# Attention over three branches: products of probabilities and values in plain float32, two heads on the halves of the array's columns

## The chip, the cores and the metric

The kernel runs on one core of a Trainium2 chip. A core has a matrix engine (TensorE; PE in the profile, PEld its weight loads) and four others: VectorE (DVE), ScalarE (ACT), GpSimd (POOL), and SyncE (SP), which here only issues DMAs. Each engine takes its instructions in the order in which the program gives them to it. The metric is the device time of one execution in microseconds, the median of the runs.

## What is computed

Two transformer blocks over 512 tokens of 1024 features, all in float32. The change touches the last attention of the second block. It has 16 heads of 64 features in four groups; the heads of a group share keys and values. Each head's result is a sum of three attentions, each times a gate of its own per token and head:

```python
o_cmp = einsum('bghqn,bngd->bqghd', p_cmp, v_cmp)     # 31 compressed blocks of the keys
o_sel = einsum('bghqkl,bgqkld->bqghd', p_sel, v_sel)  # selected blocks: with 512 keys, all of them
o_win = einsum('bghqs,bsgd->bqghd', p_w, v_w)         # the last 512 keys: all of them
out = einsum('bsch,bschd->bshd', gates, o).reshape(b, s, NSA_HEADS * DH)
return out @ w_o
```

With 512 keys, the second and the third are causal attentions over all earlier tokens, each with keys and values of its own.

## The kernel before

The weights stream in by large DMAs and are split into two parts, high and low, that TensorE's fast float32 (`float32r`) holds exactly; activations are split the same way (`split`, L542). A product of two float32 matrices is then three fast products (`group`, L556). All matmuls made by the helper `mm` bear its line, L540, so they are told apart by tiles and shapes.

The attention in question is `n_attend` (L2000). Its work is a list of steps, written out by hand: for each of four groups first one step for the compressed branch, then for each of four heads and each of two branches (`b`: selected, window) four steps, one for each chunk `c` of 128 queries in the order 3, 2, 0, 1. Chunk `c` meets 128 (c + 1) keys. That is 33 steps a group and 132 in all. A step has parts, and the table `ORDER` says how many steps after the step's scores each part is issued, and in which order the parts of different steps stand in the engines' queues:

- `scores` (L2081): two `float32r` products of queries and keys on TensorE, into one of three banks of PSUM;
- `bias` (L2089): on DVE the mask, the scale and the row's least value, into one of six buffers `np`;
- `exp` (L2097): on ACT the exponentials and their sum; `sums`: on DVE the reciprocal; `scale` (L2105): on POOL the probabilities times gate over sum;
- `turn` (L2111): on TensorE one to four transpositions, into one of four banks;
- `high` and `low` (L2119, L2128): the transposed probabilities as two parts, the high one made by ACT, the low one by DVE (tiles `pts` for branch 0, `pth` and `ptl` for branch 1);
- `out` (L2132): after a head's last chunk of a branch, eight products, four blocks of keys by two parts, 512, 384, 256 and 128 queries wide. The values stand on the 128 columns of the array as their high and low parts side by side (tile `vs`), so one product gives both. With branch 0 come two more, 512 wide, for the compressed branch (`cph`, `cpl`, `vc`). All sum up in one bank, `av`;
- `join` and `add` (L1761): ACT copies the lower half of that bank into the place of the head's queries (`h`), DVE adds the other half; `head` (L2156) makes the high part `oh` for each pair of heads. The low parts `ol` follow at the end of the stage (`lower`, L2013).

Beside the steps, `g_query` (L2054) prepares the queries of the next pair a little at each step ("tick"): a shuffle on DVE, the rotary embedding on POOL, the high part on ACT, the low part on POOL in two halves (L2075), and a DMA from SP's queue that copies them to the other half of the partitions. After the last step the output projection begins: the products of the first three pieces of the output weights (`out(k)`) are issued between the last parts of the steps.

Another place of the kernel, `g_pair` (L1013) in the first block, has plain float32 products with 64 columns of weights that go to the halves of a bank in turn (L1068, tiles `d` and `xc`).

Of the kernel before, what the change touches and what calls it, by code (L numbers as in the profile page):

```python
# [10 lines left out]
F32 = mybir.dt.float32  # L11
# [182 lines left out]
def _pcol(v):  # L194
    """A vector of 128 * n values as [128, n], value p of tile k at [p, k]."""
# [3 lines left out]
def _columns(x):  # L199
    """Per-partition columns: name -> [128, n]."""  # L200
# [25 lines left out]
def _constants():  # L226
    """Tables that depend on the shapes alone: name -> [128, n]."""
# [73 lines left out]
# ---------------------------------------------------------------- the kernel  # L301

class Weights:
    """The weight stream: large loads that run ahead, each piece split exactly in two parts."""
# [54 lines left out]
    def ahead(self):  # L359
        """The first half of what the next get() makes."""  # L360
# [10 lines left out]
class Norm:  # L371
    """One over the root of the mean square over the features, for tokens in the free dimension.

    The factor is applied to what the products give, so that they need not wait for it."""

    def __init__(self, s, eps, name, n=T, apart=False):
        """apart: the last squares are summed on their own."""
# [17 lines left out]
    def mean(self, src=None, more=None):  # L395
        """Mean squares with tokens on partitions, [128, chunks], before eps."""
# [32 lines left out]
    def bcast(self, tm=None, tag="rbc", bufs=2):  # L429
        """The factor along the free dimension, the same on every partition."""  # L430
# [13 lines left out]
class Norm2:  # L444
    """The norm that ends the first block and the one that opens the second, as one factor."""
# [22 lines left out]
class Kernel:  # L468
# [19 lines left out]
    def open_banks(self, stack, pool):  # L488
        """PSUM: a pool of eight banks, or banks by their places."""
# [66 lines left out]
    def group(self, ps, w, xh, xl, ks, first, last, m=P):  # L556
        """Accumulate into ps over the k tiles ks: three products of the parts."""
# [1695 lines left out]
```

## Time and profile before

| | |
|---|---|
| median of 3 runs (lowest, highest) | 2265.91 us (2264.5, 2266.25) |
| span of the profiled execution, first to last instruction | 2262.3 us; its own time beside the span is not given |
| PE busy | 2161.9 us (96%), 10250 instructions |
| PEld busy | 1776.0 us (79%) |
| DVE busy | 1305.9 us (58%), 2058 instructions |
| ACT busy | 910.6 us (40%), 1485 |
| POOL busy | 544.6 us (24%), 559 |
| chain that ended last, by engine | PE 68%, DVE 15%, ACT 7%, issue 5%, POOL 4%, DMA 1% |

Busy times are shares of the whole span, over stages of different kinds. A matmul's end is modelled, since matmuls are pipelined: a busy PE is not one at its peak. The chain is followed back from the last instruction, at each step to what released it. The attention that is changed begins at 1682.3 us of the span with its first scores; the first product of the output projection starts at 1850.88.

### The profile page before, as it was taken

What the parts mean: (1) busy time and instruction counts of PE and PEld (TensorE: products, weight loads), DVE (VectorE), ACT (ScalarE), POOL (GpSimd) and SP (SyncE); (2) the same over time, 40 slices, a digit from 0 to 9 for tenths busy, and PEclk for the clock granted to TensorE, in tenths of its full rate; (3) what the DMA queues carried; (4) which work ended last, traced back from release to release, by engine and by line L of the source; (5) the groups of instructions that cost most, each with busy time, mean ns of one, the idle gap of its engine ahead of it and who ended that gap; (6) DMA issues with size and microseconds to landing.
All of it is one profiled execution on the core that took longest, in us unless ns stands there. A gap on an engine that the chain in (4) does not pass through costs nothing.

```text
span 2262.3 us, 27154 instructions
## 1 busy us (share of the span) xinstructions
PE 2161.9 (96%) x10250; PEld 1776.0 (79%) x10250; DVE 1305.9 (58%) x2058; ACT 910.6 (40%) x1485; POOL 544.6 (24%) x559
## 2 busy tenths in 40 slices
PE   8899999999999999999899999999888899999998
PEld 5677888788888887777778888887677778888886
DVE  6988756454433335589965343445768875534333
ACT  4333534343322224366544332332448864423222
POOL 3333401111110104166630000013448851000001
PEclk9999999999999999999999999999899999999999
DMA  4222434122332223322233323323331113333231
GB/s 136 67 64 73 140 106 152 59 66 94 101 103 93 93 89 98 121 65 66 56 106 100 103 93 94 102 93 121 106 108 30 31 43 117 93 103 95 94 101 65
DMA packets 63379, 206.09 MB, mean 91 GB/s; under 512 B 7440, under 2 KB 8336, under 8 KB 63120
## 3 DMA queue, kind: packets, MB, share of 16 engines
q1 hardware_dynamic: 59504, 196.99, 27.8%
q10 hardware_dynamic: 3744, 7.37, 0.9%
q8 instruction: 80, 1.31, 0.2%
q14 instruction: 51, 0.42, 0.1%
HBM read 189.39 MB, written 6.29 MB: 86 GB/s over the span
## 4 chain that ended last, share of the span: by engine, by line
PE 68%; DVE 15%; ACT 7%; issue 5%; POOL 4%; DMA 1%; ACTq 0%; POOLq 0%; DVEq 0%
PE psum L540 53%; PE b L540 13%; DVE wl L350 2%; DVE spl L1718 1%; ACT wh L341 1%; DVE t L908 1%; POOL np L2108 1%; ACT sT L1670 1%; ACT sT L1671 1%; DVE pv L1089 1%; DVE xl L553 1%; POOL cx L1832 1%; PE psum L2116 1%; ACT xh L552 1%; DVE pts L2130 1%
## 5 line engine op out<-in xcount | busy, mean ns | idle before, releaser
L540 PE MATMUL psum<-xh,wh 128*128 128x512 f32 x1560 | 611.6, 392 | 2.3 <-ACT sA L1725 1.3
L540 PE MATMUL psum<-xh,wl 128*128 128x512 f32 x1560 | 609.4, 391 | 1.8 <-DVE wl L350 1.5
L540 PE MATMUL psum<-xl,wh 128*128 128x512 f32 x1560 | 608.8, 390 | 0.0
L341 ACT ACTIVATE wh<-ws 128x1024 fp32r<-128x1024 f32 (+1 forms) x346 | 356.3, 1038 | 384.8 <-PE psum L540 321.5
L350 DVE TENSOR_TENSOR wl<-ws,wh 128x1024 fp32r<-128x1024 f32 (+2 forms) x332 | 421.1, 1274 | 86.1 <-ACT wh L341 85.4
L540 PEld LDWEIGHTS psum<-xh,wl 128*128 128x128 f32 x1560 | 293.1, 188 | 66.3 <-DVE wl L350 4.3
L540 PEld LDWEIGHTS psum<-xh,wh 128*128 128x128 f32 x1560 | 293.3, 188 | 63.4 <-issue 1.8
L540 PEld LDWEIGHTS psum<-xl,wh 128*128 128x128 f32 x1560 | 293.3, 188 | 60.9 <-DVE xl L550 0.2
L540 PE MATMUL b<-xh,wh 128*128 128x512 f32 (+1 forms) x488 | 196.1, 402 | 8.4 <-ACT wh L341 6.6
L540 PE MATMUL b<-xh,wl 128*128 128x512 f32 (+1 forms) x488 | 193.6, 397 | 3.8 <-POOL wl L350 1.9
L540 PE MATMUL b<-xl,wh 128*128 128x512 f32 (+1 forms) x488 | 193.7, 397 | 0.5 <-DVE xl L553 0.5
L1357 DVE TENSOR_TENSOR h<-h,psum 128x512 f32<-128x512 f32 x48 | 33.1, 689 | 161.2 <-PE psum L540 161.2
L540 PE MATMUL psum<-hh,wh 128*128 128x512 f32 x320 | 125.1, 391 | 0.0
L540 PE MATMUL psum<-hh,wl 128*128 128x512 f32 x320 | 124.7, 390 | 0.0
L540 PE MATMUL psum<-hl,wh 128*128 128x512 f32 x320 | 124.6, 389 | 0.0
L1348 ACT ACTIVATE t<-t 128x512 f32<-128x512 f32 x64 | 40.5, 632 | 188.9 <-DVE t L1347 188.9
L540 PEld LDWEIGHTS b<-xh,wh 128*128 128x128 f32 (+1 forms) x488 | 92.9, 190 | 28.4 <-ACT wh L341 6.6
L540 PEld LDWEIGHTS b<-xh,wl 128*128 128x128 f32 (+1 forms) x488 | 92.8, 190 | 26.6 <-DVE wl L350 3.3
L553 DVE SCALAR_TENSOR_TENSOR xl<-h,cols,xh 128x512 fp32r<-128x512 f32 x64 | 76.6, 1212 | 61.9 <-ACT xh L552 61.9
L540 PEld LDWEIGHTS b<-xl,wh 128*128 128x128 f32 (+1 forms) x488 | 92.9, 190 | 20.5 <-DVE xl L553 1.2
L392 POOL TENSOR_TENSOR acc_final<-acc_final,sq_final 128x512 f32<-128x512 f32 x6 | 10.4, 1733 | 336.1 <-ACT sq_final L388 336.1
L1287 POOL TENSOR_TENSOR t<-t,t 128x512 f32<-128x512 f32 x22 | 28.4, 1290 | 257.2 <-DVE t L1282 232.7
(515 smaller groups left out, 3510.6 us busy)
## 6 DMA issues: line engine op xcount, KB each, us to landing
ws<-in_wst SPq DMA_DIRECT2D x332, 512.0 KB, 3.4
h<-in_xT SPq DMA_DIRECT2D x16, 256.0 KB, 3.7
kk<-kk SPq DMA_DIRECT2D x16, 256.0 KB, 3.4
nq<-nq SPq DMA_DIRECT2D x16, 256.0 KB, 2.9
ws<-in_wst SPq DMA_DIRECT2D x8, 384.0 KB, 3.1
spill<-back SPq DMA_DIRECT2D x8, 256.0 KB, 2.0
back<-spill ACTq DMA_DIRECT2D x8, 256.0 KB, 3.5
spill<-h ACTq DMA_DIRECT2D x8, 256.0 KB, 5.9
```

What stands on the lines that cost most here:

```text
L341: self.nc.scalar.activation(hi[:, :n], s, AF.Copy)
L350: e.tensor_tensor(lo[:, :n], s, hi[:, :n].bitcast(F32), op=ALU.subtract)
L540: self.nc.tensor.matmul(ps, a, b, start=start, stop=stop, skip_group_check=again)
L552: nc.scalar.activation(hi, src, AF.Copy, scale=scale)
L553: nc.vector.scalar_tensor_tensor(lo, src, scale, hi.bitcast(F32), op0=ALU.mult, op1=ALU.subtract)
L908: nc.vector.scalar_tensor_tensor(t, u[:, q:q + T], cw[:, q:q + 1], t, op0=ALU.mult, op1=ALU.add)
L1089: nc.vector.tensor_tensor(o[:, a:], src[:, a:], src[:, a - n:528 - n], op=ALU.add)
L1287: nc.gpsimd.tensor_tensor(t, t, gate[0], op=ALU.mult)
L1348: nc.scalar.activation(t, t, AF.Square)
L1357: nc.vector.tensor_tensor(self.h[:, m, :], self.h[:, m, :], ps, op=ALU.add)
L1670: self.nc.scalar.activation(t, t, AF.Exp)
L1671: self.nc.scalar.activation(t, t, AF.Ln, bias=1.0)
```

## The change

The products of probabilities and values become plain float32 products: the values are held once (64 columns), the probabilities too, and the two heads of a pair go to the two halves of the array's columns, and so to the halves of the bank `av`. The steps of a pair are put in the order branch, head, chunk, so that the two heads' probabilities of a branch are there together, and `out` is issued for both after the second head's last chunk. The transposed probabilities are copied out of PSUM once instead of split: chunks 3 and 0 by ACT, chunks 2 and 1 by DVE; three buffers take turns, one of them in the rest of the values' slab. A pair's result is split into `oh` and `ol` straight from the bank; joins, additions and the low parts at the end go. The low parts of the queries are made by DVE, in one instruction a head, instead of POOL in two. The compressed branch and the values before the steps lose their parts as well. The rest of the diff takes comments and docstrings out.

```diff
-        vs = self.slab("vs").rearrange("p k t -> p (k t)").rearrange(
-            "p (b c g d) -> p b c g d", b=2, c=4, g=4)
+        half = self.slab("vs", F32).rearrange("p k t -> p (k t)")
+        vs = half[:, :2048].rearrange("p (b c g d) -> p b c g d", b=2, c=4, g=4)
+        self.pt0 = half[:, 2048:3712].rearrange("p (n q) -> p n q", q=P)
...
         for c, ps in enumerate(pss):
-            o = self.vs[:, :, c, :, :]
-            v = ps.rearrange("p (b g d) -> p b g d", b=2, g=4)
-            for b in range(2):
-                self.split(o[:, b, :, 0:64], o[:, b, :, 64:128], v[:, b], norm.tm[:, c:c + 1])
+            nc.scalar.activation(self.vs[:, :, c, :, :],
+                                 ps.rearrange("p (b g d) -> p b g d", b=2, g=4), AF.Copy,
+                                 scale=norm.tm[:, c:c + 1])
...
-    ORDER = (("scores", 0), ("out", 7), ("join", 9), ("bias", 1), ("turn", 4), ("exp", 2), ("add", 9),
-             ("sums", 2), ("low", 6), ("tick", 0), ("high", 5), ("scale", 2), ("head", 13))
+    ORDER = (("scores", 0), ("out", 7), ("head", 9), ("bias", 1), ("turn", 4), ("exp", 2),
+             ("sums", 2), ("tick", 0), ("move", 5), ("scale", 2))
...
-            for h in range(4 * g, 4 * g + 4):
+            for h0 in (4 * g, 4 * g + 2):
                 for b in range(2):
-                    for c in self.QORD:
-                        steps.append(dict(g=g, h=h, b=b, c=c))
+                    for h in (h0, h0 + 1):
+                        for c in self.QORD:
+                            steps.append(dict(g=g, h=h, b=b, c=c))
...
-            if 0 <= j < 7:
-                lower(j)
-        lower(7)
...
             nc.scalar.activation(q[r, 0, :], qr[r, :], AF.Copy)
-            for s in halves:
-                nc.gpsimd.tensor_tensor(q[r, 1, s], qr[r, s], q[r, 0, s].bitcast(F32),
-                                        op=ALU.subtract)
-                yield
+            yield
+            nc.vector.tensor_tensor(q[r, 1, :], qr[r, :], q[r, 0, :].bitcast(F32),
+                                    op=ALU.subtract)
+            yield
...
-    def n_high(self, u):
+    def n_move(self, u):
...
+            self.pt[h, b] = self.pt0 if self.npt % 3 == 2 else self.tmp("pt", (P, 13, P), bufs=2)
+            self.npt += 1
+        dst = self.pt[h, b][:, c:4 * c + 1:3, :]
+        src = u.pop("ps")[:, :P * (c + 1)].rearrange("p (j q) -> p j q", q=P)
+        if c in (1, 2):
+            self.nc.vector.tensor_copy(dst, src)
+        else:
+            self.nc.scalar.activation(dst, src, AF.Copy)
...
-        if u["c"] != self.QORD[3]:
+        if u["c"] != self.QORD[3] or h % 2 == 0:
             return
-        pt = self.pt.pop((h, b))
+        halves = [slice(0, 64), slice(64, 128)]
         if b == 0:
             self.av = self.bank("av")
             cp, vc = self.cp
-            for part in cp:
-                self.mm(self.av, vc[:, h % 4, :], part, part is cp[0], False)
+            for e in range(2):
+                self.mm(self.av[halves[e]], vc[:, (h - 1 + e) % 4, :], cp, True, False)
+        pt = [self.pt.pop((h - 1 + e, b)) for e in range(2)]
         for j in range(4):
-            for part in pt:
-                self.mm(self.av[:, P * j:], self.vs[:, b, j, g, :],
-                        part[:, 4 * j:3 * j + 4, :].rearrange("p c q -> p (c q)"),
-                        False, b == 1 and j == 3 and part is pt[1])
+            for e in range(2):
+                self.mm(self.av[halves[e], P * j:], self.vs[:, b, j, g, :],
+                        pt[e][:, 4 * j:3 * j + 4, :].rearrange("p c q -> p (c q)"),
+                        False, b == 1 and j == 3)
...
             p = u["h"] // 2
-            self.nc.scalar.activation(self.oh[:, p, :], self.qraw[:, p, :], AF.Copy)
+            self.split(self.oh[:, p, :], self.ol[:, p, :], self.av)
```

## Rows read from the trace of the kernel before

**Rows 1.** Window: stretch, us, then busy us (instructions) of PE PEld DVE ACT POOL.

```profile
1718.02:1759.89 41.87, 36.84 (x239) 29.97 (x238) 37.04 (x145) 36.93 (x109) 34.96 (x55) 1.00 0.13 28
```

**Rows 2.** Waits of three groups: who waited for whom, us in total, times, longest.

```profile
PEld psum L2116 <- POOL np L2108: 15.2, 30, 0.8
DVE nsm L2103 <- ACT np L2099: 11.8, 15, 1.2
...
PEld psum L540 <- DVE pts L2130: 5.8, 12, 1.1
...
PEld psum L2116 <- POOL np L2208: 3.7, 3, 1.2
PEld psum L540 <- DVE ptl L2130: 3.3, 9, 0.7
```

**Rows 3.** DVE groups by shape, same stretch: busy us, mean ns, idle.

```profile
L2130 DVE TENSOR_TENSOR pts<-psum,pts 128x512 fp32r<-128x512 f32 x13 | 8.7, 673 | 0.0
...
L2130 DVE TENSOR_TENSOR pts<-psum,pts 128x384 fp32r<-128x384 f32 x12 | 6.5, 538 | 0.0
...
L2130 DVE TENSOR_TENSOR pts<-psum,pts 128x256 fp32r<-128x256 f32 x12 | 4.8, 403 | 0.0
...
L2130 DVE TENSOR_TENSOR pts<-psum,pts 128x128 fp32r<-128x128 f32 x12 | 3.2, 268 | 0.0
...
L1765 DVE TENSOR_TENSOR h<-h,psum 64x512 f32<-64x512 f32 x12 | 8.1, 678 | 0.5 <-ACT h L1764 0.3
```

**Rows 4.** ACT groups by shape, same stretch.

```profile
L2126 ACT ACTIVATE pts<-psum 128x384 fp32r<-128x384 f32 x13 | 6.1, 471 | 0.0
...
L2126 ACT ACTIVATE pts<-psum 128x256 fp32r<-128x256 f32 x12 | 4.6, 381 | 0.2
```

**Rows 5.** POOL groups by shape, same stretch.

```profile
L2075 POOL TENSOR_TENSOR nq<-qr,nq 64x256 fp32r<-64x256 f32 x23 | 16.8, 729 | 1.0
```

**Rows 6.** DVE groups, whole span: copies, subtractions on 64 partitions.

```profile
L941 DVE COPY btm<-b 128x384 f32<-128x384 f32 x2 | 1.1, 548 | 0.0
...
L1869 DVE COPY hidt<-psum 128x256 f32<-128x256 f32 x2 | 0.8, 411 | 0.0
...
L1455 DVE TENSOR_TENSOR sq<-st,sq 64x512 fp32r<-64x512 f32 x16 | 11.0, 686 | 1.2 <-ACT sq L1453 0.7
...
L1455 DVE TENSOR_TENSOR ks<-nkr,ks 64x512 fp32r<-64x512 f32 x8 | 7.6, 953 | 0.2
```

**Rows 7.** Timeline of DVE in the drain: start us, us of the piece.

```profile
1848.39 0.67 DVE L2014 TENSOR_TENSOR ol<-h,oh 128x512 fp32r<-128x512 f32 x1
1848.99 0.54 DVE L2130 TENSOR_TENSOR ptl<-psum,pth 128x384 fp32r<-128x384 f32 x1
```

**Rows 8.** Timeline of POOL, same moment.

```profile
1848.51 1.97 POOL L2108 TENSOR_SCALAR np<-np,nsm,gates 128x128 f32<-128x128 f32 x2
```

**Rows 9.** Timeline of PE: plain float32, 16 columns of the array, four products.

```profile
74.87 1.04 PE L540 MATMUL b<-small,adt 128*16 128x128 f32 x8
```

**Rows 10.** Timeline of PE: plain float32, halves of the columns, eight products (L1068).

```profile
99.23 0.39 PE L540 MATMUL b<-xl,wh 128*128 128x512 f32 x1
99.46 0.39 PE L540 MATMUL b<-xh,wl 128*128 128x512 f32 x1
99.78 1.09 PE L540 MATMUL b<-d,xc 128*64 128x128 f32 x16
100.80 0.94 PE L540 MATMUL b<-ct,prev 128*128 128x128 f32 x6
```

**Rows 11.** Timeline of PE: one head's products with the values, and what follows.

```profile
1777.62 0.39 PE L540 MATMUL psum<-cph,vc 128*128 128x512 f32 x1
...
1778.08 1.41 PE L540 MATMUL psum<-pts,vs 128*128 128x512 f32 x8
1779.32 0.30 PE L2116 MATMUL psum<-small,np 128*128 128x128 f32 x1
```

**Rows 12.** Timeline of PE in the drain.

```profile
1847.27 0.50 PE L540 MATMUL psum<-cph,vc 128*128 128x512 f32 x1 [1.46 <-DVE h L1765]
```

More of the change, by code (lines that the diff above doesn't have):

```diff
@@ L1797, in _nsa @@
         ):
-            self.oh = self.slab("oh")
-            pts = self.slab("pts").rearrange("p k t -> p (k t)")
-            self.pts = [pts[:, 1664 * a:1664 * a + 1664].rearrange("p (n q) -> p n q", q=P)
-                        for a in range(2)]
+            self.oh, self.ol = self.slab("oh"), self.slab("ol")
             self.n_attend()
@@ L1885, in second @@
                 self.mm(ps[:, :64], ht[:, e, :], w2[:, 1, e, :], e == 0, e == 1)
-            v = self.vcs
-            nc.scalar.activation(v[:, 0:64], ps[:, :64], AF.Copy)
-            nc.vector.tensor_tensor(v[:, 64:], ps[:, :64], v[:, 0:64].bitcast(F32),
-                                    op=ALU.subtract)
+            nc.scalar.activation(self.vcs, ps[:, :64], AF.Copy)
     def n_proj(self, norm, xh, xl):
@@ L2004, in n_attend @@
             steps.append(dict(g=g, c=3))
-            for h in range(4 * g, 4 * g + 4):
+            for h0 in (4 * g, 4 * g + 2):
                 for b in range(2):
-                    for c in self.QORD:
-                        steps.append(dict(g=g, h=h, b=b, c=c))
+                    for h in (h0, h0 + 1):
+                        for c in self.QORD:
+                            steps.append(dict(g=g, h=h, b=b, c=c))
         n = len(steps)
-        self.pt = {}
+        self.pt, self.npt = {}, 0
         lead = []
-        def lower(p):
-            self.nc.vector.tensor_tensor(ol[:, p, :], self.qraw[:, p, :],
-                                         self.oh[:, p, :].bitcast(F32), op=ALU.subtract)
+        ol = self.ol
         def out(k):
@@ L2139, in n_out @@
             cp, vc = self.cp
-            for part in cp:
-                self.mm(self.av, vc[:, h % 4, :], part, part is cp[0], False)
+            for e in range(2):
+                self.mm(self.av[halves[e]], vc[:, (h - 1 + e) % 4, :], cp, True, False)
+        pt = [self.pt.pop((h - 1 + e, b)) for e in range(2)]
         for j in range(4):
-            for part in pt:
-                self.mm(self.av[:, P * j:], self.vs[:, b, j, g, :],
-                        part[:, 4 * j:3 * j + 4, :].rearrange("p c q -> p (c q)"),
-                        False, b == 1 and j == 3 and part is pt[1])
-    def n_join(self, u):
-        if u["b"] == 1 and u["c"] == self.QORD[3]:
-            u["add"] = self.join(u["h"], self.av, self.qraw[:, u["h"] // 2, :])
-    def n_add(self, u):
-        if "add" in u:
-            u["add"]()
+            for e in range(2):
+                self.mm(self.av[halves[e], P * j:], self.vs[:, b, j, g, :],
+                        pt[e][:, 4 * j:3 * j + 4, :].rearrange("p c q -> p (c q)"),
+                        False, b == 1 and j == 3)
     def n_head(self, u):
@@ L2171, in c_scores @@
                         self.kb[:, g, pr, :], pr == 0, pr == 1)
-        vc = u["vc"] = self.tmp("vc", (P, 4, P), F32R, bufs=2)
-        nc.gpsimd.memset(vc.bitcast(F32), 0.0)
+        vc = u["vc"] = self.tmp("vc", (P, 4, 64), bufs=2)
+        nc.gpsimd.memset(vc, 0.0)
         for h in range(4):
-            nc.sync.dma_start(out=vc[32 * h:32 * h + 32, h, :].bitcast(F32),
-                              in_=self.vcs[32 * g:32 * g + 32, :].bitcast(F32))
+            nc.sync.dma_start(out=vc[32 * h:32 * h + 32, h, :],
+                              in_=self.vcs[32 * g:32 * g + 32, :])
     def c_bias(self, u):
@@ L2212, in c_turn, with c_move @@
         self.n_turn(u)
-    def c_high(self, u):
-        u["parts"] = [self.tmp("cp" + a, dtype=F32R, bufs=1) for a in "hl"]
-        self.nc.scalar.activation(u["parts"][0], u["ps"], AF.Copy)
-        u["cp"] = u["parts"], u.pop("vc")
-    def c_low(self, u):
-        self.n_low(u)
+    def c_move(self, u):
+        cp = self.tmp("cp", bufs=1)
+        self.nc.scalar.activation(cp, u.pop("ps"), AF.Copy)
+        u["cp"] = cp, u.pop("vc")
     def c_out(self, u):
```

12 lines of the change are left out of this document (1 added, 11 removed).

## The prediction

> **What bounds the kernel now.** I read the page first: TensorE is busy nearly all of the span, and its matmuls make up most of the chain that ended last, so a change that takes work from the other engines pays only where TensorE waits for them. The table of 40 slices shows one long stretch where POOL, ACT and DVE are all high at once: the attention of the second block, the only stage that the change touches in earnest. There I cut windows. The stage is four groups of four heads (33 steps each), and the chain of waits shows the same products starting again after 41.87 us, three times, with the same counts of instructions and busy times within 0.1 us in the second and the third window. In such a window DVE is busy 37.05 us, ACT 36.9, POOL 34.95; TensorE shows 36.9, but with the modelled ends of pipelined matmuls [rows 1]. No engine is full, three are close to it. The waits of three groups say how they hold each other: the weight loads of the transposes wait 15.2 us for POOL's scaling, those of the value products 5.8 us for DVE's low parts, 3.7 us more for the compressed branch, together 24.7, so 8.2 us a group; DVE in turn waits 11.8 us for ACT's exponentials [rows 2]. So TensorE's own load lies between 41.87 - 8.2 = 33.7 and 36.9 us a group. The stage is a pipeline of in-order engines about two steps apart, DVE and ACT the fullest, and its period is DVE's 37.05 plus 4.8 us of idle time. After the stage the output projection runs on TensorE without a gap; what is gained before it is kept.
>
> **DVE, a group.** Removed: 8 times (4 heads, 2 branches) the low parts of four chunks, 0.673 + 0.538 + 0.403 + 0.268 = 1.88 us, so 15.1; four additions that join halves, 0.678 each, 2.7; the low part of the compressed probabilities, 512 columns, 0.67 [rows 3]. That is 18.4 us in 37 instructions. Added: 8 copies of 384 and 8 of 256 columns out of PSUM, for which the same shapes elsewhere show 0.548 and 0.411, so 7.7; the low parts of four heads' queries, 64 x 512, which come from POOL, 0.686 each, 2.7 [rows 6]; two low parts of a head pair's result, which used to be made in the drain, 0.67 each, 1.3 [rows 7]. That is 11.7 in 22. Neighbours on DVE overlap by 0.07 (a piece of 0.67 that starts at 1848.39, the next at 1848.99 [rows 7]), so 15 instructions fewer give back 1.0. DVE falls by 5.7, to 31.4.
>
> **ACT and POOL, a group.** ACT loses the high parts of two of four chunks, 8 x (0.471 + 0.381) = 6.8 [rows 4], and four evacuations of 512 columns that fed the joins, at least as long as the 384's 0.47, 1.9; less 20 overlaps of 0.07, some 7.3, to 29.6. POOL loses 8 x 0.729 = 5.8 [rows 5], to 29.1. The query parts keep their ticks and their place in SP's queue; the DMA now waits for DVE instead of POOL.
>
> **The query parts beside POOL.** A DVE subtraction with two SBUF inputs took 0.67 while POOL was scaling [rows 7, 8], yet the keys' 64 x 512 subtractions average 0.953 against 0.686 for the same shape in the first attention [rows 6]. I take 0.686; the other end is 4 x 0.27 = 1.1 us a group. The Trainium skill (GPSIMD Engine Reference, Specifications) has POOL's SBUF interface shared with VectorE, in contention with DVE instructions of two SBUF inputs. By that rule these four would be slow and POOL with them, 1.1 us a group; the row beside POOL's scaling shows nothing of it.
>
> **TensorE, a group.** A head's products with the values of one branch and of the compressed one take from 1777.62 to 1779.32, 1.70 us, of which the compressed branch's two 512-column products are 2 x 0.23 (the spacing 99.23 to 99.46); the other branch's burst is 1.24 [rows 10, 11]. For a pair of heads: 2 x 1.70 + 2 x 1.24 = 5.9. Afterwards every product is plain float32, which the profile lists twice: four products on 16 columns of the array are 8 records in 1.04 us, 0.13 each [rows 9]. On the two halves of the columns, in the same alternating order as the new code, 16 records take 1.02 us from 99.78 to 100.80, 0.064 each [rows 10]: the halves run side by side. So 128 columns of one head cost 1.02 / 8 = 0.128, changing to halves and back included; a burst of two heads is 2 x 1280 / 128 = 20 such units, 2.55 us, at the most, since a burst of 1.02 pays for the change as one of 2.5 does. The stream before it ran at 0.23 a product, and the first half product came 0.32 after the last full one: 0.09 for the change. Taking twice 0.09 off the 1.02 leaves 0.105 a unit, so 2.1 + 0.2 = 2.3 at the least; I take 2.4. The compressed branch adds 8 units, 0.9. A pair: 2 x 2.4 + 0.9 = 5.7 against 5.9. TensorE's load stays.
>
> **What is late next.** The bursts come half as often and twice as long, 3.3 and 2.4 us by turns, and scores and transposes queue behind them on TensorE; DVE waits for both. DVE has about two steps in hand, 2 x 31.4 / 33 = 1.9 us, so a pair may leave it idle for 1.4 + 0.5 us, up to 3.8 a group, and nothing if TensorE is further ahead; I take 1.5. Second, the low part of a pair's result now stands on DVE right behind its high part on ACT, with the next masked scores queued behind it; before, other work lay between. DVE's waits for ACT go up to 1.2 [rows 2]; twice 0 to 1.2 a group, I take twice 0.7.
>
> **The sum.** Period 31.4 + 4.8 (today's idle time) + 1.5 + 1.4 = 39.1, 2.8 less than 41.87; four groups give 11.1. In the drain TensorE waits 1.46 for a join before the last head's products [rows 12]; that goes, and I count 1.0, since POOL's and ACT's latencies stay. The profiled span is 2262.3, so 2250.2; its execution's own time is not on the page, and the median of the runs, 2265.9, lies 3.6 above the span. Keeping that: 2254 us, 0.5% faster. The value evacuations in the projection before (8 pairs of parts become 4 copies) and the smaller clears and copies lie under TensorE's work: nothing, unless a value copy is late by its 0.5.
>
> **Rivals.**
> A, TensorE becomes the bound and the longer bursts eat the gain: the idle time grows to 9.5 to 11 us, period 41 to 42.4, time 2262 to 2268, no difference that can be told. For: its load of 33.7 to 36.9 is above DVE's new 31.4. Against: it has slack for 5 us, and the buffers for scores and transposes still hold two steps.
> B, the gain comes whole: fewer waits between ACT and DVE as both get lighter, idle time 4 or less, period 35 to 36.5, so -21 to -28: 2238 to 2245.
> C, slower: the halves run one after the other where the products are 512 to 128 columns wide and add onto a sum, unlike the 128-column ones that stand alone. A unit then costs 0.22 to 0.26, each burst about 2.2 more, the compressed part 0.9: 4 x 2.2 + 2 x 0.9 = 10.6 us a group, load 44 to 47. It decides once the load passes 41.87; at 45.5 a period, 2280. The Trainium skill (FP8 and Floating Point Precision, TensorE Precision Notes) counts four passes for true float32. By that rule alone the products double and C holds; the records on 16 columns agree with it (0.26 a product of 128 columns), and only the halves' overlap in the mixer stands against it [rows 9, 10].
> D, the change doesn't overlap because a half's products wait for the other's in the queue: the same place as C with half its price, load 39 to 42, time as in A.
>
> **How the numbers follow.** A measurement tells 0.2%, 4.5 us, from nothing here. Likeliest, 2246 to 2260: 0.53. B 0.18. A and D together 0.18, of which a third ends just beyond 4.5 us on either side. C 0.08; other mishaps 0.03. Faster: 0.53 + 0.18 + 0.05 = 0.76; same 0.14; slower 0.10. The range leaves out the lower part of B and what lies above A: 2240 to 2265.
>
> **What would show it.** Steps at 39 us a group instead of 41.87; DVE's busy time near 31 in a group's window and ACT's near 30; a pair's burst of 16 records about 2.4 us long, records of the two halves starting together; transposes waiting less for POOL; new idle time of DVE behind ACT's high part of the result. The prediction is wrong if a burst is 4 us or longer (C), if the period stays above 41 with DVE at 31 (A), or if DVE's copies out of PSUM cost more than the parts they replace.

## The result, and the profile after

The changed kernel takes 2275.17 us (median of four runs, 2274.41 to 2280.23) against 2266.08 for the kernel before (2264.5 to 2266.64): a ratio of 1.0051, 95% interval 1.0038 to 1.0063. It is slower by 0.4 to 0.6%; 2254 had been forecast, 0.5% faster.

The page is much as before (busy us, share of the span, instructions):

```profile
PE 2170.8 (95%) x10250; PEld 1762.7 (77%) x10250; DVE 1276.0 (56%) x1981; ACT 880.7 (39%) x1401; POOL 524.8 (23%) x527
```

The attention is where the time went. Windows show it best when they are cut by its own work. Each of the following begins at the exponential of every eighth step, so four of them make a group, the last with the compressed branch's step. Columns are the stretch, its length, then busy us (instructions) of PE, PEld, DVE, ACT and POOL, the granted clock (1.00 is 2.4 GHz), and the DMAs' share and GB/s. First the third group before the change, which [rows 1] shows as a whole for another group:

```profile
1767.68:1777.91 10.23, 8.32 (x58) 6.99 (x57) 10.03 (x40) 8.32 (x26) 7.98 (x12) 1.00 0.01 3
1777.91:1788.07 10.16, 8.88 (x55) 6.80 (x54) 7.87 (x34) 9.69 (x30) 9.22 (x15) 1.00 0.24 52
1788.07:1797.25 9.18, 8.64 (x57) 7.17 (x56) 8.77 (x37) 8.21 (x26) 7.82 (x13) 1.00 0.01 4
1797.25:1809.54 12.29, 11.09 (x73) 9.02 (x72) 10.39 (x38) 10.72 (x32) 9.91 (x16) 1.00 0.21 45
sum 41.86, PE 36.94 PEld 29.97 DVE 37.06 ACT 36.93 POOL 34.93; mean PE 9.23 PEld 7.49 DVE 9.27 ACT 9.23 POOL 8.73
```

And after the change the same four quarters, from the second and third group, each where TensorE ran at 2.4 GHz all through:

```profile
1775.44:1785.94 10.50, 8.16 (x55) 5.72 (x55) 8.23 (x36) 7.32 (x23) 7.87 (x13) 1.00 0.01 2
1743.78:1753.82 10.04, 8.49 (x56) 5.63 (x56) 7.32 (x32) 7.47 (x22) 7.29 (x11) 1.00 0.24 54
1753.82:1762.86 9.04, 8.67 (x56) 5.71 (x55) 6.96 (x32) 6.73 (x23) 7.95 (x13) 1.00 0.00 1
1762.86:1775.44 12.58, 10.59 (x73) 7.58 (x72) 9.38 (x34) 8.18 (x24) 7.29 (x12) 1.00 0.21 45
sum 42.16, PE 35.90 PEld 24.64 DVE 31.88 ACT 29.71 POOL 30.39; mean PE 8.98 PEld 6.16 DVE 7.97 ACT 7.43 POOL 7.60
```

DVE has lost 5.2 us of work a group, ACT 7.2 and POOL 4.5 (forecast 5.7, 7.3 and 5.8), and yet no quarter is more than 0.14 us shorter. At full clock the period is 42.16, not 39.1: the gain is missing already here. The clock comes on top. The same quarters elsewhere in the same execution, with the same work:

```profile
1730.45:1743.78 13.33, 10.99 (x55) 7.30 (x55) 8.45 (x36) 7.30 (x23) 7.85 (x13) 0.74 0.00 1
1805.08:1819.22 14.14, 12.13 (x73) 8.75 (x72) 9.33 (x34) 8.19 (x25) 7.31 (x12) 0.88 0.18 40
```

The granted clock fell to 1.2 GHz for half of the first and a quarter of the second, which cost 13.33 - 10.50 = 2.8 and 14.14 - 12.58 = 1.6 us. Each of the two comes twice, 8.8 us in this execution; before the change the clock was full from 1691 to 1848, nearly the whole stage. The two profiled spans differ by 16.1 us: 2.1 lie before the stage's first exponential, 11.4 between its first and its last (these 8.8 among them), 0.7 are won back in the drain, and 3.3 come after the first product of the output projection, with the clock at 1.2 GHz for 6.8 us from 1862.1 (before the change for 3.5 from 1848.2). The profiled execution was the longest of the four (2280.23, mean clock 0.978 over the span); the others have 0.980 and 0.981 and 2274.4 to 2275.7, the kernel before 0.985 in its profile.

Next, the sizes that the prediction took from single rows. These are groups of instructions in the stretch of three groups, 1725.72 to 1858.25 (line, engine, shapes, count | busy us, mean ns):

```profile
L2116 DVE COPY pt<-psum 128x384 f32<-128x384 f32 x16 | 8.7, 546 | 4.3 <-PE psum L2105 4.2
L2064 DVE TENSOR_TENSOR nq<-qr,nq 64x512 fp32r<-64x512 f32 x10 | 6.9, 685 | 0.2
L2116 DVE COPY pt<-psum 128x256 f32<-128x256 f32 x16 | 6.5, 406 | 0.0
L2097 POOL TENSOR_SCALAR np<-np,nsm,gates 128x512 f32<-128x512 f32 x24 | 20.5, 856 | 5.7 <-DVE nsm L2092 4.4 <-PE psum L2105 1.0 <-DVE nmx L2083 0.3
```

The copies (0.546, 0.406) and the queries' low parts (0.685) are as forecast from [rows 6] to 0.005 us; these parts of the sum stand. POOL's scaling of 512 columns, 0.856 us on average, was 0.769 before; the last section comes back to it. A pair's burst, from the timeline of PE (start, length, instructions):

```profile
1766.76 1.08 PE L540 MATMUL psum<-cp,vc 128*64 128x512 f32 x4
1767.66 2.32 PE L540 MATMUL psum<-pt,vs 128*64 128x512 f32 x16
1769.92 0.33 PE L2105 MATMUL psum<-small,np 128*128 128x128 f32 x1
```

From 1766.76 to 1769.92 are 3.16 us with the compressed branch, 0.9 and 2.26 (forecast 0.9 and 2.4). The halves run side by side at 512 to 128 columns too, and rival C is out. The Trainium skill (FP8 and Floating Point Precision, TensorE Precision Notes) counts four passes for true float32; by that alone, an estimate, this burst would have been about twice as long. The waits of three groups, which answer to [rows 2] (waiting, waited for: us, times, longest):

```profile
POOL np L2097 <- DVE nsm L2092: 31.9, 33, 3.2
PEld psum L2105 <- POOL np L2097: 22.4, 34, 1.4
...
DVE nsm L2092 <- ACT np L2088: 15.2, 34, 1.5
...
ACT pt L2118 <- PE psum L2105: 11.3, 8, 3.0
```

Before the change, POOL's wait for DVE over three groups was:

```profile
POOL np L2108 <- DVE nsm L2103: 11.3, 19, 1.8
```

TensorE's weight loads wait more for POOL than before (22.4 against 15.2), POOL for DVE (31.9 against 11.3), DVE for ACT (15.2 against 11.8), and ACT's copies now wait for TensorE's transposes (11.3 in this row): engines with less to do wait for one another in a circle. The stretch after the change holds three falls of the clock, which lengthen some of these waits. The chain of waits shows the step of the compressed branch between two groups (start, us, what):

```profile
1766.59 3.40 PE psum L540 x22
1769.99 0.26 PE psum L2105
1770.25 0.24 PE psum L540 x2
1770.49 0.22 PE psum L2105 x2
1770.71 1.80 PE psum L540 x16
...
1772.60 0.70 DVE np L2169
...
1773.33 0.70 DVE cmx L2171
...
1774.83 0.64 ACT np L2176
...
1775.49 0.69 DVE csm L2181
...
1777.06 1.06 POOL np L2190
...
1778.16 0.66 PE psum L2105 x4
```

Behind the burst of 3.16 us come the compressed scores, then DVE, ACT, DVE and POOL one after the other, 7.4 us from the scores to the end of the scaling. Apart from one reciprocal of a masked step (0.17 us) the chain has no other work in that time.

### The profile page after: what moved, and what is told of

It is laid out like the page before. It is cut to its first block, busy times and chain, and to the rows that moved or that the text cites. A ratio compares the mean times of both kernels' runs of the same rounds, so it can differ in the third digit from the quotient of the medians.

```text
span 2278.4 us, 26846 instructions
## 1 busy us (share of the span) xinstructions
PE 2170.8 (95%) x10250; PEld 1762.7 (77%) x10250; DVE 1276.0 (56%) x1981; ACT 880.7 (39%) x1401; POOL 524.8 (23%) x527
## 4 chain that ended last, share of the span: by engine, by line
PE 69%; DVE 14%; ACT 7%; issue 5%; POOL 4%; DMA 0%; ACTq 0%; POOLq 0%; DVEq 0%; SPq 0%
PE psum L540 54%; PE b L540 13%; DVE wl L350 2%; PE psum L2105 1%; DVE spl L1718 1%; ACT wh L341 1%; DVE t L908 1%; ACT sT L1670 1%; ACT sT L1671 1%; POOL np L2097 1%; DVE pv L1089 1%; DVE xl L553 1%; POOL cx L1830 1%; DVE sT L1665 1%; ACT xh L552 1%
## 5 line engine op out<-in xcount | busy, mean ns | idle before, releaser
L2097 POOL TENSOR_SCALAR np<-np,nsm,gates 128x512 f32<-128x512 f32 (+3 forms) x128 | 83.4, 655 | 48.4 <-DVE nsm L2092 36.4
L2105 PE MATMUL psum<-small,np 128*128 128x128 f32 x336 | 66.5, 302 | 26.8 <-POOL np L2097 18.5
```

Of the source, the lines that this page charges most:

```text
L2097: self.nc.gpsimd.tensor_scalar(u["p"], u["p"], u.pop("sm"), self.gates[:, u["c"], e:e + 1], op0=ALU.mult, op1=ALU.mult)
L2105: self.nc.tensor.transpose(ps[:, s], p[:, s], self.ident)
```

## The experiments

Eighteen kernels were run, each against the kernel before on the same chip. That kernel's medians lay between 2263.9 and 2266.1, so times from different chips compare to about 2 us. Theory 1 is bursts in TensorE's queue, 2 the clock, 3 the chain over ACT, DVE and POOL; a later theory is told in the expectation that brings it in. The cuts of code show the changed places only.

**Bursts in four pieces.**

```diff
-("out", 7), ("head", 9)
+("cmp", 6), ("out0", 7), ("out1", 8), ("out2", 9), ("out3", 10), ("head", 12)
```

> A pair's products with the values are issued in four pieces, one key chunk at a step (7, 8, 9 and 10 steps after the scores), the compressed branch's two products one step before them; the result's parts follow 3 steps later than now. Nothing is left out. Theory 1 (the long bursts stand in TensorE's queue ahead of scores and transposes, and nothing else has enough in hand): the group's long steps (2.1 to 4.3 us where a burst stands, against 1.2 on average) shrink, the period at full clock falls from 42.2 to 39 to 40.5 and the time to 2258 to 2266. Theory 2 (the loss is the granted clock, which was at 1.2 GHz for 20.5 us in the middle of the stage, against none there before): only if the clock's drops go away does the time fall, and then by the 9 us that they cost, to about 2266; if they stay, 2272 to 2277. Theory 3 (the chain from ACT's exponential over DVE's reciprocal and POOL's scaling sets the step, the bursts are incidental): no change, 2272 to 2278.

2276.69 us, ratio 1.005 (1.0037 to 1.0063): no gain. It told little, since a new wait came in: the last piece is read in the step in which its buffer is filled again, and ACT's copies waited for TensorE's products 11.8 us in two groups, up to 3.1 at once.

**One step deeper.**

```diff
-("out", 7), ("head", 9), ("turn", 4), ("sums", 2), ("move", 5), ("scale", 2)
+("out", 8), ("head", 10), ("turn", 5), ("sums", 3), ("move", 6), ("scale", 3)
```

> One step more between the exponentials and the reciprocals and scaling, and so for the transposes, the moves, the products with the values and the result's parts (lags 3, 5, 6, 8 and 10 in place of 2, 4, 5, 7 and 9). Nothing is left out. Theory 1 (bursts in TensorE's queue): transposes and moves then run a step (1.3 us) further behind, which covers part of a burst but not the scores behind it: 2266 to 2273. Theory 2 (clock): 2272 to 2278, with about 20 us at 1.2 GHz in the stage. Theory 3 (the chain over ACT, DVE and POOL sets the step): a step more in it takes DVE's waits for ACT away, 15.2 us over three groups for the reciprocals; the period falls by 3 us or more, to 2262 or less.

2265.28, ratio 1.0005 (0.9997 to 1.0014): some 10 us of the changed kernel's time are gone. The second group:

```profile
1727.16:1768.75 41.59, 36.61 (x237) 24.69 (x237) 31.30 (x130) 28.76 (x89) 30.62 (x46) 1.00 0.12 27
```

It took 41.59 at full clock, against 42.16: 0.6 a group, which is not 10 us in four groups. The rest goes with the clock, which is low in the stage only for 3.4 us in its third group and where the stage begins. The time lies just below theory 1's range; theory 3's period was not reached.

**Low parts of the queries back on POOL.**

```diff
-            yield
-            nc.vector.tensor_tensor(q[r, 1, :], qr[r, :], q[r, 0, :].bitcast(F32),
-                                    op=ALU.subtract)
-            yield
+            for s in halves:
+                nc.gpsimd.tensor_tensor(q[r, 1, s], qr[r, s], q[r, 0, s].bitcast(F32),
+                                        op=ALU.subtract)
+                yield
```

> The low parts of the queries go back from DVE to POOL, in halves, as before the change; all else as after it. Nothing is left out. Theory 1 (bursts): POOL gets 5.8 us a group back and DVE loses 2.7; neither is full, the bursts stay, so 2273 to 2281. Theory 4 (DVE's 64 x 512 subtractions and the high part's own tick, which delays the second head's queries by a step, are what costs): 2264 to 2270.

2277.86, ratio 1.0058 (1.0045 to 1.0072). Taking this edit of the change back gained nothing; theory 4 falls.

**Few products.**

```diff
-        for j in range(4):
+        for j in (3,):
```

> Leaves out the products with the values of the first three of four key chunks, 12 of a pair's 16 a group and branch pair; a burst falls from 20 units of two halves (2.4 us) to 2, the compressed branch's 8 stay. All copies, scalings and transposes stay. It prices the bursts. Theory 1: with bursts of 0.3 and 1.2 us the stage is held by DVE's 32 us and its waits for ACT, period 36 to 38, time 2250 to 2258. Theory 2 (clock): TensorE does less, so the clock drops more often, and what the products give back goes to it: 2262 to 2275. Theory 3: the chain over ACT, DVE and POOL is unchanged, period 42 or more, 2266 to 2276.

2257.59, ratio 0.9967 (0.9955 to 0.998). A group of it (columns as above):

```profile
1726.00:1765.87 39.87, 30.40 (x188) 22.18 (x188) 31.75 (x129) 29.23 (x90) 30.32 (x47) 0.96 0.13 28
```

With most of the bursts gone the period is still 39.87, at a clock of 0.96, above the 39.1 of the forecast. Theory 1 asked for 36 to 38 and is half wrong: the products left out cost at least 2.3 us a group (the clock is lower here), and without them something else holds the step, though DVE is idle for 8 of 39.9 us. The clock fell more often than before the change, as theory 2 has it, yet the time fell further than it allowed.

**The compressed step inside the group before, and a step deeper.**

```diff
+            if g == 0: steps.append(dict(g=g, c=3))
...
+                            if g < 3 and len(steps) == 33 * g + 28:
+                                steps.append(dict(g=g + 1, c=3))
```

> The version that is one step deeper, and beside that the compressed branch's step of groups 2 to 4 goes from between the groups into the group before, ahead of its last five steps. Nothing is left out. There its scores' 16 records (1.79 us) follow the 3.16 us burst on TensorE at once, and its 7 instructions on DVE (2.7 us) fall into the same place: the two steps around it take 4.9 and 0.7 to 1.8 us. Theory 1 (what stands together in TensorE's queue sets the long steps): apart from the burst, 2 to 3 us a group come back, the time falls from 2265 to 2256 to 2261. Theory 3 (DVE's and ACT's own work for that step sets it wherever it stands): no change, 2263 to 2268.

2254.05, ratio 0.9953 (0.9941 to 0.9966): faster than the kernel before.

```profile
1763.98:1772.63 8.65, 8.55 (x59) 6.00 (x57) 6.79 (x33) 6.46 (x21) 8.02 (x13) 1.00 0.01 2
1772.63:1781.98 9.35, 8.58 (x54) 5.32 (x53) 7.07 (x32) 7.12 (x22) 6.58 (x10) 1.00 0.26 58
1781.98:1790.69 8.71, 8.59 (x59) 5.98 (x57) 6.79 (x33) 6.46 (x21) 8.07 (x13) 1.00 0.00 1
1790.69:1802.48 11.79, 10.20 (x73) 7.44 (x73) 10.21 (x39) 8.45 (x24) 7.67 (x12) 1.00 0.22 49
```

Every quarter is shorter, the group 38.50, and the clock is full. In the chain the compressed step now takes 1.9 us of scores and three instructions of DVE, and then it leaves it for the masked scores; its sums and its scaling are no longer on it:

```profile
1752.32 1.93 PE psum L540 x16
...
1754.38 0.69 DVE np L2172
...
1755.09 0.70 DVE cmx L2174
...
1756.12 0.02 DVEq L2086
...
1756.75 0.95 POOL np L2100
...
1757.75 0.55 PE psum L2108 x3
```

**Scores two steps ahead, and a step deeper.**

```diff
+("out", 9), ("head", 11), ("bias", 2), ("turn", 6), ("exp", 3), ("sums", 4), ("move", 7), ("scale", 4)
```

> The version that is one step deeper, and beside that the masked scores, and all that follows them, come one step later: the scores run two steps ahead of DVE on their three banks in place of one. Nothing is left out. Theory 1 (scores that queue behind a burst leave DVE idle: 10 us over two groups in the version that is one step deeper, for the masked scores of both kinds, and as much again by POOL behind it): a step more in hand takes most of it, 2255 to 2261. Theory 3 (the chain from the exponential to the scaling, or the transposes, is what is short): 2263 to 2268. A loss (2268 or more) would say that the banks for the scores are then the wait.

2275.31, ratio 1.0045 (1.0033 to 1.0058): worse than the deeper version by 10 us. The waits of one group say why; they are waits that the changed kernel hardly has:

```profile
PEld psum L540 <- DVE nmx L2083: 12.2, 14, 1.4
...
PE psum L540 <- DVE nmx L2083: 8.8, 10, 1.2
```

With three banks filled two steps ahead, TensorE waits at the next scores until DVE has emptied a bank, and what stands behind them in its queue waits too. The group took 44.8 us with no fall of the clock.

**All three, with pieces.** The last two edits together, and the burst as the compressed products, key chunks 0 and 3, then 1 and 2:

```diff
-("out", 9), ("head", 11)
+("cmp", 8), ("outa", 9), ("outb", 10), ("head", 12)
```

> All three: a step deeper, the scores two steps ahead, the compressed branch's step inside the group before; and a pair's burst in three pieces, the compressed branch's products one step before, key chunks 0 and 3, then 1 and 2 a step later. Nothing is left out. Here the last piece is read two steps before the buffer of the probabilities is filled again (in the version in four pieces it was the same step, and the moves waited for it). Theory 1: with no piece longer than 1.2 us and two steps in hand, the period comes near DVE's 32 us plus its waits for ACT, 36 to 38, and the time to 2245 to 2254. Theory 3: the chain over ACT, DVE and POOL keeps 39.8, the period of the version with few products: 2256 to 2260.

2262.0, ratio 0.9982 (0.9974 to 0.9991). That is above both ranges. The version of 2251 below differs from it only in having the scores one step ahead, so they cost 11 us here too.

**First product of the scores twice.**

```diff
+        self.mm(u["ps"][:, :w], q[:, 0, P * c:P * c + P], k[:, :w], True, True)
```

> The changed kernel, and each step's first product of the scores is given twice (its first giving is overwritten; nothing is left out): TensorE has 0.1 to 0.2 us more at each step, 5 us a group. Theory 2 (TensorE's idle time behind the bursts lets the granted clock fall, and that costs 9 us of the profiled execution): the drops to 1.2 GHz in the stage go away or get rarer, 20.5 us to 7 or less, and the time falls to 2266 to 2273. Theory 1 (the queue on TensorE is what binds): every step has 0.16 us more in that queue, 128 of them: 2276 to 2290 whatever the clock does.

2280.03, ratio 1.0065 (1.0052 to 1.0079), 5 us more than the changed kernel; the low clock shrank to 6.8 us inside the stage, and the time still rose. At full clock its third group took 44.02 us, 1.9 more than 42.16, with 4.1 us more of TensorE's work (39.98 against 35.90). Work on TensorE costs time there; the clock alone doesn't set it.

**Deeper, compressed step moved, bursts in pieces.** The version of 2254, and its last piece two steps clear of the buffer's refilling:

```diff
-("out", 8), ("head", 10)
+("cmp", 7), ("outa", 8), ("outb", 9), ("head", 11)
```

> The version that is one step deeper with the compressed branch's step inside the group before (2254), and its bursts in pieces: the compressed branch's products one step ahead, key chunks 0 and 3 where the burst is now, 1 and 2 a step later, the result's parts a step later too. Nothing is left out. Theory 1 (bursts in TensorE's queue bind): no piece is longer than 1.2 us in place of 2.3 and 3.16; the period falls from 38.5 towards 36, the time to 2244 to 2251. Theory 3 (with a step more in hand the bursts are covered, and the chain over ACT, DVE and POOL binds): 2252 to 2256. Theory 5 (what counts is how much TensorE has to do between two waits, and more switches between halves and the full array cost more than they spread): 2256 to 2262.

2251.03 (2250.45 to 2254.12), ratio 0.9944 (0.9931 to 0.9956): the fastest. Its period is 37.75. The pieces bring 3 us over the same version without them (2254.05), with intervals that overlap, so theory 1 holds here weakly at most.

**Only the compressed step moved.** The list of steps as in the version of 2254, all lags the changed kernel's:

```diff
+                            if g < 3 and len(steps) == 33 * g + 28:
+                                steps.append(dict(g=g + 1, c=3))
```

> The changed kernel with its own lags, and only the compressed branch's step moved into the group before. Nothing is left out. Theory 1 (two things that each ask for slack: the bursts for one step more, the compressed step for a place away from them): alone it brings what it brought the deeper version, 11 us, or less: 2263 to 2269. Theory 6 (it pays only once the pipeline is a step deeper, since the waits behind the bursts are the same as before): 2272 to 2277.

2264.3, ratio 1.0003 (0.9994 to 1.0012), 11 us less than the changed kernel: theory 6 falls, the place counts by itself.

```profile
1726.90:1767.39 40.49, 37.06 (x237) 25.41 (x236) 32.05 (x131) 29.53 (x89) 30.43 (x46) 1.00 0.13 28
```

**The kernel before, one step deeper.**

```diff
-("out", 7), ("join", 9), ("turn", 4), ("add", 9), ("sums", 2), ("low", 6), ("high", 5), ("scale", 2), ("head", 13)
+("out", 8), ("join", 10), ("turn", 5), ("add", 10), ("sums", 3), ("low", 7), ("high", 6), ("scale", 3), ("head", 14)
```

> The kernel before the change, one step deeper in the same way (reciprocals and scaling 3 steps after the scores, transposes 5, high and low parts 6 and 7, products 8, joins 10, the result's high part 14). Nothing is left out. Theory 1 (the change's bursts, twice as long, are what asks for a step more; bursts of 1.2 to 1.7 us are covered): 2262 to 2267, no change from before. Theory 3 (the chain from the exponential to the scaling is short of a step in both kernels, and the change only brings no relief to it): 2252 to 2260, as much as the changed kernel gained by it.

2267.59, ratio 1.0013 (1.0004 to 1.0022): nothing gained, slightly lost. Depth pays only after the change.

**The result's low part a step later**, in the version of 2254.

```diff
-("head", 10)
+("head", 10), ("hlow", 11)
```

> The version of 2254 (a step deeper, the compressed step inside the group before), and a pair's low part of the result one step after its high part in place of right behind it. Nothing is left out. In that version DVE waits 7.5 us for ACT's high part over two groups, in four waits. Theory 7 (that wait is on the path, as the prediction had it at 1.4 us a group): 3 us a group come back at the most, 2243 to 2251. Theory 1 (DVE waits there because TensorE's burst holds ACT too; without that wait the masked scores behind it wait for TensorE instead): 2252 to 2256.

2253.48, ratio 0.9951 (0.9937 to 0.9964): no change, theory 7 falls. DVE's wait for ACT's high part (7.5 us in two groups) is gone, and its wait for the scores on TensorE rose from 5.3 to 11.9 in the same stretch.

**Only the bursts in pieces**, at the changed kernel's own lags.

```diff
-("out", 7), ("head", 9)
+("cmp", 6), ("outa", 7), ("outb", 8), ("head", 10)
```

> The changed kernel with its own lags and order, and only the bursts in pieces: the compressed branch's products 6 steps after the scores, key chunks 0 and 3 after 7, 1 and 2 after 8; the result's parts after 10. The last piece is read two steps before its buffer is filled again (in the version in four pieces it was the same step). Nothing is left out. Theory 1 (length of the burst): pieces of 1.2 us in place of 2.3 and 3.16 are what the kernel before had (1.24 and 1.7), so its period or less, 40 to 41.5, and 2260 to 2267. Theory 6 (not the length but the place beside the compressed step and the depth): 2271 to 2277.

2276.57, ratio 1.0054 (1.004 to 1.0068). Clean of the buffer wait, and no gain: the length of the burst alone is not the cause.

**Transposes ahead of the burst.**

```diff
-("scores", 0), ("out", 7), ("head", 9), ("bias", 1), ("turn", 4)
+("scores", 0), ("head", 9), ("bias", 1), ("turn", 4), ("out", 7)
```

> The changed kernel with its own lags, and only the order within a step changed: the transposes stand ahead of the products with the values in TensorE's queue, so that the burst delays the next step's scores but not this step's transposes. Nothing is left out. Theory 8 (the loss comes by the transposes: the copies, with the exponentials queued behind them on ACT, wait for those that stand behind a burst): 2262 to 2269. Theory 9 (it comes by the scores that wait, which are behind the burst in both orders): 2272 to 2277; and if transposes ahead of the burst wait for POOL's scaling and hold the burst up, more than that.

2276.24, ratio 1.0044 (1.0031 to 1.0058). Theory 8 falls. The five executions line up with their clocks: 2271.5 twice at 0.983, 2276.2 and 2276.3 at 0.980, 2278.7 at 0.978.

**The fastest version with transposes first.**

```diff
-("cmp", 7), ("outa", 8), ("outb", 9), ("head", 11), ("bias", 1), ("turn", 5)
+("head", 11), ("bias", 1), ("turn", 5), ("cmp", 7), ("outa", 8), ("outb", 9)
```

> The fastest version so far (2251: a step deeper, the compressed step inside the group before, the bursts in pieces), and the transposes ahead of the pieces in each step. Nothing is left out. Theory 8: 2246 to 2250. Theory 9: 2250 to 2256.

2261.21, ratio 0.9981 (0.9972 to 0.999): 10 us worse than without, beyond both ranges. DVE's wait for the scores on TensorE rose from 3.4 to 13.4 us in the same stretch; that transposes which wait for POOL hold TensorE up is argued from this, not shown.

**Only the compressed transposes two steps later.**

```diff
+("cturn", 6), ("cmove", 7)
```

> The changed kernel with its own lags; only the compressed branch's transposes and their copy come 6 and 7 steps after its scores in place of 4 and 5. Nothing is left out. Theory 10 (the compressed step's serial chain over DVE, ACT, DVE and POOL, 7.4 us from its scores to its scaling, is longer than the four steps after which TensorE's queue holds its transposes, 4.7 us at the mean step; TensorE waits there and everything behind it): 1.5 to 2.5 us a group, and less time at the low clock: 2262 to 2268. Theory 11 (the chain is long, but what counts is DVE's and ACT's queue that it blocks, the transposes only show it): 2271 to 2277.

2280.98, ratio 1.007 (1.0058 to 1.0083), six runs from 2274.27 (clock 0.983) to 2283.01 (0.978). Theory 10 falls: it isn't TensorE's wait at those transposes.

**The same in the fastest version (first line), and in the kernel before (second).**

```diff
+("cturn", 7), ("cmove", 8)
...
+("clow", 8), ("chigh", 7), ("cturn", 6), ("cout", 9)
```

> The fastest version so far (2251: a step deeper, the compressed step inside the group before, the bursts in pieces), and its compressed transposes and their copy two steps later, 7 and 8 after the scores. Nothing is left out. Theory 10: the last long steps, 3.7 and 2.3 us around the compressed step, shrink by 1 to 2 us a group, 2243 to 2248. Theory 11: 2249 to 2254.

> The kernel before the change; only the compressed branch's transposes and its high and low parts come 6, 7 and 8 steps after its scores in place of 4, 5 and 6. Nothing is left out. Theory 10, if the bound was there before the change: 1 to 2 us a group, 2257 to 2262. If DVE and ACT, both busy 37 of 41.9 us, are what set that kernel's pace: 2263 to 2268.

2252.41, ratio 0.9946 (0.9935 to 0.9958), and 2266.36, ratio 1.0005 (0.9996 to 1.0013). No change in either.

## Why the prediction was wrong

**The step that failed** is the first term of the sum after DVE's work: "Period 31.4 + 4.8 (today's idle time)". It read the period as DVE's busy time plus a rest that stays. DVE's busy time fell nearly as forecast, to 31.9, and its idle time rose by as much, from 4.8 to 42.16 - 31.88 = 10.3. The quarters of the kernel before already hint at it: in its second and third DVE was idle for 2.3 and 0.4 us, yet after the change, with 0.6 and 1.8 us less on DVE, they last within 0.14 us as long. The waits argue that what holds the stage is the circle between engines only a step or two apart, and a circle's length isn't any engine's load. Of the 21.2 us between forecast and measurement, 4 x (42.16 - 39.1) = 12.2 are the period's and 0.3 the drain's; of the 8.7 that are left, some 4 to 8 are the clock's by the estimate below.

The prediction's "late next" terms don't fill this gap. The bursts, taken at 1.5 a group, gave back 2.3 or more when most of their products were left out, and nothing when they were cut in pieces; and the period without those products was still 39.87, where the sum without its 1.5 has 37.6. The wait for the result's high part was sized right (1.4 a group; 4.4 us in three groups) but wasn't on the path where that was tried, in the version of 2254: taken away, it moved to the scores.

**What is late instead** was not in the prediction: the compressed branch's step, 7.4 us in series, that begins behind the burst of 3.16 us at each change of group. Moved away from it, with nothing else changed, it gave 11 us; a step more in hand gave 10; both gave 21. Not all of this is the period. From the stage's first exponential to its last, the profiled executions of the changed kernel, the deeper one, the one with the step moved, and the one with both took:

```profile
1686.88:1860.15 173.27, 148.49 (x903) 102.42 (x903) 122.66 (x502) 116.09 (x347) 116.52 (x176) 0.92 0.11 24
1686.02:1847.95 161.93, 143.59 (x898) 97.10 (x899) 120.20 (x503) 112.52 (x346) 117.86 (x175) 0.97 0.12 26
1685.05:1843.84 158.79, 143.47 (x903) 98.17 (x903) 122.87 (x502) 115.56 (x347) 116.73 (x176) 0.98 0.12 27
1685.76:1836.65 150.89, 139.75 (x898) 96.42 (x899) 118.87 (x503) 111.55 (x346) 116.96 (x175) 0.98 0.12 28
```

All four have 6.8 us of low clock at their start. The later falls cost 8.8 us in the first and 1.6 in the second (a quarter of 11.33 against 9.72 at full clock), and the last two have none. Without them the gains are 4.2 us for the depth, 5.7 for the place and 13.6 for both: together more than one by one, and a period of 38.50, which is where the forecast (39.1) had put it. The rest of the 10, 11 and 21 us goes with the clock.

In the kernel before, the deeper pipeline gave nothing: there DVE and ACT have 37 of 41.9 us to do. So the change did free engines, and the schedule written for their old loads could not use it. By which queue the compressed step holds the others is not settled. Its transposes aren't it (three runs). What remains is its scores on TensorE, 1.8 us that start 0.8 after the burst, or DVE's seven and POOL's one instruction, in order with the masked steps; the move took both from that place at once, and no run separates them.

**The clock** was not in the prediction either, and it makes a loss out of a period that hardly moved. The pairs of equal quarters price a fall at 1.6 and 2.8 us. Over whole executions of one kernel, 0.003 to 0.005 of mean clock go with 4.7 to 7.2 us (transposes first), 0.002 to 0.003 with 4.5 to 5.8 (the changed kernel). The changed kernel's three shorter executions have 0.980 to 0.981, the kernel before 0.985 in its profile and 0.984 by the median of 83 later executions; at the slope of the first, an estimate, some 4 to 8 of the 9 us are the clock's. The period at full clock (42.16 against 41.86) gives 4 x 0.3 = 1.2. What makes it fall is open: it stayed full in versions with a period of 38.5 and of 44.8, and fell in the one of 39.9 with few products.

**What was right.** DVE's and ACT's work, TensorE's (35.90 for 36.94 before) and the burst; the halves side by side; nothing from the value evacuations (the stage's first exponential comes 2.1 us later, with the clock at 1.2 GHz just before it; where it fell later, with the queries on POOL, it comes at 1684.37, before the change at 1684.77). From the last exponential to the first product of the output projection it is 3.5 us against 4.2, so 0.7 of the 1.0 forecast for the drain. Rival A named the right period (41 to 42.4), and its sign came true (above 41 with DVE near 31), but its reason holds in part at most: TensorE's load did not rise, and cutting its products still left 39.9. The only rival on the slower side, C, priced a thing that didn't happen. The chance of a slower kernel, 0.10, had no case for waits that grow as loads fall.

**Two rows misread.** POOL's load was off by 1.3 (30.4 for 29.1). The prediction took nothing for POOL from the query parts, since "the row beside POOL's scaling shows nothing of it". That row [rows 8] is two scalings, of 128 and of 256 columns, in 1.97 us; elsewhere in the stage they take 0.446 and 0.555, so it did show it. And TensorE's waits in [rows 2] are 28.0 us with the 3.3 for `ptl`, not 24.7, which lowers the bound on its load from 33.7 to 32.5; no term of the sum uses it.

## What to carry to other kernels

Where three in-order engines are each busy 83 to 89% of a period and none is full, do not take the period as the fullest one's work plus a fixed rest: compare stretches of the period in which that engine's share differs, and if their lengths don't follow it, the pace is likely a chain between engines, and less work may move nothing until lags and places are set anew. Price falls of the clock apart from the period, by equal stretches at full clock. After relieving engines, try one step more of depth and another place for the odd step (here 10 and 11 us, 24 with bursts in pieces, to 2251.03, 0.56% below the kernel before), and check that a longer lag doesn't run into a buffer's refilling or fill all banks ahead.

## What the runs showed of the hardware

- Plain float32 products on the two halves of the array's columns overlap at each of the four widths: 16 records of 512 to 128 columns took 2.26 us, and the records of the two halves start 6 to 8 ns apart.
- POOL's scaling slowed where VectorE subtracted two SBUF inputs. The average of 0.856 us for 128x512, against 0.769 before the change, hides two kinds: in three groups nineteen of 24 kept 0.77, and five took 1.19, each beginning under a subtraction of the queries' low parts; five of the 128-column ones took 0.75 in place of 0.45 beside the other five subtractions. That is 1.2 us a group. With those subtractions back on POOL, all 24 averaged 0.767. The subtractions themselves kept their 0.685. The Trainium skill (GPSIMD Engine Reference, Specifications) has POOL's SBUF interfaces shared with VectorE, in contention with instructions of two SBUF inputs. The trace agrees for POOL (1.19 against 0.77) and shows no cost on VectorE's side here. One pair after the change, and the row with the subtractions on POOL:

```profile
1750.11 0.69 DVE L2064 TENSOR_TENSOR nq<-qr,nq 64x512 fp32r<-64x512 f32 x1
1750.25 1.19 POOL L2097 TENSOR_SCALAR np<-np,nsm,gates 128x512 f32<-128x512 f32 x1 [0.44 <-DVE nsm L2092]
...
L2097 POOL TENSOR_SCALAR np<-np,nsm,gates 128x512 f32<-128x512 f32 x24 | 18.4, 767 | 3.7 <-DVE nsm L2092 2.2 <-PE psum L2105 1.0
```

- Executions of one kernel on one chip differ by up to 8.7 us (2274.27 and 2283.01), and their mean granted clocks (0.983 and 0.978) differ with them.
